# Other places for the split weights of the merge stage, unread products at the start, and some loads issued earlier or by another queue

## The chip, the cores and the metric

The kernel runs on one core of a Trainium2 chip. PE multiplies: a matmul takes a stationary operand of 128 x 128, its weights, which a weight load (PEld in the profile) brings in beforehand, and streams a moving operand of up to 512 columns past it into a PSUM bank. DVE and ACT do elementwise work, POOL and SP mostly issue DMAs here. Each engine works through its own list of instructions in order, and semaphores tie the lists together. The order on each list is not written by hand throughout: a scheduler makes it when the program is built, from the order of the Python calls and from which operands it expects to be ready.

The metric is the device time of one execution in microseconds (us). The kernel before takes 2859.32 us, the median of 3 runs (2859.23 to 2859.35).

## The reference

One encoder block over 512 tokens of 2048 channels, all in float32. Cut to what matters here:

```
hn = rmsnorm(x, norm1_w);  proj = hn @ w_in            # 2048 -> 11280 columns
conv_out = centred_depthwise_conv(proj[:, :5120])
y_a = hyena(conv_out[:, :3072])          # long convolutions with a learned filter
y_b = sigmoid(o) * mlstm_both_directions(q, k, v, gates)
gate_a, gate_b = sigmoid(merge[:, :2048]), sigmoid(merge[:, 2048:])
mixed = gate_a * (y_a @ w_branch_a) + gate_b * (y_b @ w_branch_b)
x = x + mixed @ w_out
gu = rmsnorm(x, norm2_w) @ w_gate_up
x = x + (silu(gu[:, :5632]) * gu[:, 5632:]) @ w_down
return rmsnorm(x, norm_f_w)
```

`merge` is the last 4096 columns of `proj`. It is 16 groups of 256 columns, and these groups are the merge stage.

## The kernel before

**Products in float32 by splitting.** Every operand is split into a high part, rounded to the type that PE takes in one pass (F32R), and a low part, the remainder. A product is three matmuls: high x high, high x low, low x high (`mm3`, L78 to L81, all through `mm`, L75 to L76). A split is an ACT copy (the high part) and a DVE subtraction (the low part): L176 and L177 in `split_w`, L1105 and L1106 in the class `Winograd`, L86 and L87 in `split`.

**Stages, in order.** At the start `x` is loaded, transposed by PE and split into the 16 pairs of `X` (pool `ap`, tiles `a`). Then the main stream works through the columns of `w_in` in groups of 256 (`w_in_cols`), with matmuls of 512 columns. Beside it runs a side stream, of which `drive` takes a few pieces at each tick of the main stream: the Hyena convolutions (`hyena`), the mLSTM heads (`mlstm`) and the filter spectra. The merge stage follows, then `branch_a` and `branch_b`, the output projection, the gate-up stage and the down projection.

**The start** (L304 to L349). `x` comes in five pieces of columns (256, 256, 512, 512, 512), each in four tiles `xt`, all loaded by SP's queue. The first weights (`raws`, tiles `wr` of 512 KB, L169) stand in the same queue behind pieces 0, 2 and 3. `x_block(kb)` transposes one block of 128 columns (L320) into a PSUM tile `sd`, `x_split` scales and splits it (L326, L327), and after every two blocks one unit of the first column group runs, 12 matmuls of 512 columns. The pool of `sd` tiles has four buffers.

**Heads and convolutions.** `stream_a` runs `hyena(0)`, `hyena(1)`, `mlstm(0)`, `hyena(2)`, `hyena(3)` and then heads 1 to 3. A head runs eight units, one for each direction and block of 128 tokens; each makes its weights by ACT, a mask on POOL (`affine_select`, L955), DVE and ACT again. `hyena(q)` takes tiles that were fetched ahead if there are any (`fetched`); otherwise it issues four loads from `d_hy` on POOL's queue (`fetch`, L823) and pauses for two ticks. Its first PE work is the transposes of `by_times` (L759). A head fetches the `q` and `k` of the next head at its sixth unit (`following`); `mlstm(0)` is called without it.

**The merge stage.** `Winograd.cols` makes 256 columns in seven products of 8 x 3 matmuls of 256 columns, 168 in all. It takes a weight block apart into quarters, makes four sums of quarters (`add`, L1122), and splits every quarter and sum that a product needs, in two tiles of 4 x 128 columns each. So a group has 14 pairs of split tiles and 8 sum tiles. The moving operands are the tiles `a` and the combinations `T` (pool `ts`).

**Where the tiles lie.** Pools on the left side are laid one above the other from low addresses, those on the right side are counted down from the top, which stands 32 bytes below a multiple of 64. The left pools of this stage, `wp` (tiles `wr`, `wh`, `wl`), `ap` and `ts`, start at multiples of 64 bytes. All the tiles of the stage are 2048 or 4096 bytes in a partition (`xo`, `bt` and `tt` included), so those on the right lie at 32 modulo 64. In the merge stage before, split tiles are taken in turn: four pairs in `wp` (`wh`, `wl`), then two in right pools of their own (`h`, `l`); the sums are six tiles `s` on the right. The gate-up stage is the same class; there pools named `tpx`, `w2x` and `h2x`, which hold nothing, move the `T` tiles 32 bytes up against the split weights, which are four pairs in `wp` and one more.

The right pools of the merge stage take over the memory of the pool `pr`, whose tiles the column groups and the side stream use (`g`, `st`, `pp`). A new tile waits until the tiles under it have been used for the last time (`reuse_waits="tile"`). The last group ahead of the merge stage, `o_cols`, stores two `st` tiles to `d_o` by POOL's queue (L457).

**`branch_a`** loads, once per group, one tile of `d_yb` and one of `d_o` by SP's queue (`load_tile`, L1255), multiplies them a group later and splits them for `branch_b`.

Of the kernel before, what the change touches and what calls it, by code (L numbers as in the profile page):

```python
# [8 lines left out]
F32 = mybir.dt.float32  # L9
# [25 lines left out]
def hybrid_block_kernel(ctx, tc, x, norm1_w, w_in, conv_w, conv_b, filt_w1, filt_b1, filt_freq1,  # L35
# [268 lines left out]

    pieces = [(0, 256), (256, 256), (512, 512), (1024, 512), (1536, 512)]
    xt = [[new(xp, f"xt{c}_{tb}", (P, n)) for tb in range(4)] for c, (_, n) in enumerate(pieces)]
    raws = []
    for c, (c0, n) in enumerate(pieces):
        for tb in range(4):
            nc.sync.dma_start(xt[c][tb], x2d[tb * P:(tb + 1) * P, c0:c0 + n])  # L310
        if c in (0, 2, 3):
            raws.append(load_a(w_in, len(raws) * L, 0))
    first_group = group_feat(w_in, 0, KB, 0, X, raws)

    def x_block(kb):
        ps = sd_ps()
        c = max(i for i, (c0, _) in enumerate(pieces) if c0 <= kb * P)
        k0 = kb * P - pieces[c][0]
        for tb in range(4):
            nc.tensor.transpose(ps[:, tb * P:(tb + 1) * P], xt[c][tb][:, k0:k0 + P], ident)  # L320
        return ps

    def x_split(kb, ps):
# [3 lines left out]
        nc.vector.scalar_tensor_tensor(l, ps, n1[:, kb:kb + 1], h.bitcast(F32), ALU.mult, ALU.subtract)  # L327
        X[kb] = (h, l)

    for kb in range(0, KB, 2):  # L330
        blocks = [x_block(kb), x_block(kb + 1)]
        if kb == 0:
            small_columns()
        if kb:
            next(first_group)
        for k in range(2):
            x_split(kb + k, blocks[k])
# [550 lines left out]
    def mlstm(h, following=None):  # L888
# [82 lines left out]
        for n, (d, jb) in enumerate(units):  # L971
            if n == 4:
                W = {}
            if n == 5 and ("qk", following) in done:
                fetched_qk[following] = fetch_qk(following)
            W[jb] = nxt
            if n < 7:
                nxt = weights(*units[n + 1], row if n < 3 else row_b)
# [32 lines left out]
    def stream_a():  # L1011
        yield from gate_rows()
        yield from need("filter")
        for kind, n in (("hy", 0), ("hy", 1), ("hd", 0), ("hy", 2), ("hy", 3)):
            yield from hyena(n) if kind == "hy" else mlstm(n)
        ph_cm.__exit__(None, None, None)
        ts_pool.append(ts_cm.__enter__())
        done.add("ts")
        for h in (1, 2, 3):
            yield from mlstm(h, h + 1)  # L1020

    def stream_b():
        yield from filter_net()
# [200 lines left out]
        n_tile[0] += 1  # L1224
        return sx.tile(list(shape), F32, tag="bt", name=f"bt_{n_tile[0]}", bufs=4)

    wm_cm = {t: tc.tile_pool(name="wm" + t, bufs=b, side="right", reuse_waits="tile") for t, b in (("r", 4), ("s", 6), ("h", 2), ("l", 2))}
    wm = {t: cm.__enter__() for t, cm in wm_cm.items()}
    d_g = [[dram(f"d_g{k}_{b}") for b in range(16)] for k in range(2)]

# [4 lines left out]
    def ring(tag, shape, dt, own, pool, extra, more):  # L1235
# [7 lines left out]
            return new(pool, extra, shape, dt)  # L1243
        return take

    merge = Winograd(
        w_in, XT, ring("wr", (P, 4, 256), F32, 3, wm["r"], "r", 4),
        ring("wh", (P, 4, P), F32R, 4, wm["h"], "h", 2), ring("wl", (P, 4, P), F32R, 4, wm["l"], "l", 2),
        lambda: new(wm["s"], "s", (P, 4, P)), xo, lambda: bt((P, 256)))

    ya, yb = [], []

# [16 lines left out]
            nc.scalar.activation(C[j], C[j], AF.Sigmoid)  # L1269
            nc.gpsimd.dma_start(dst[j], C[j])  # L1270

    for t in ("l", "h", "s", "r"):
        wm_cm[t].__exit__(None, None, None)
    ts_cm.__exit__(None, None, None)
    pg_cm = tc.tile_pool(name="pg", bufs=20, reuse_waits="tile")
# [11 lines left out]
    def branch_a():  # L1287

        raw = []

        def put_yb():
            t, o = raw.pop(0)
            nc.vector.tensor_tensor(t, t, o, ALU.mult)
            yb.append(split(py, "y", t))

        for g in range(8):
            gates_g = [gate_tile(0, 2 * g + j) for j in range(2)]
            for r in group_feat(w_branch_a[0], 0, 8, g * 256, ya):
                if r is None:
                    yield  # L1300
            for j in range(2):
                nc.vector.tensor_tensor(gates_g[j], r[j], gates_g[j], ALU.mult)
                acc.append(gates_g[j])
            if raw:
                put_yb()
            raw.append((load_tile(d_yb, g, nc.sync), load_tile(d_o, g, nc.sync)))
        put_yb()

    mixed = []
# [295 lines left out]
```

## Time and profile before

| | |
|---|---|
| median of the timed runs | 2859.32 us |
| the profiled execution | 2869.02 us |
| its span, first to last instruction | 2867.3 us |
| DVE, busy | 2104.9 us |
| ACT, busy | 1273.0 us |
| POOL, busy | 186.2 us |
| mean granted TensorE clock | 0.998 |

The profile comes from one execution of its own, which is some 10 us longer than the timed runs. Times inside it are counted from its first instruction. A row of the timeline gives the start, the time of one stretch of like instructions, engine, line, operation, the tiles (written <- read) and, in brackets, how long the engine idled before and what ended that wait. The starts of two matmul rows tell what the matmuls between them cost; a row's own time holds the length of the pipeline as well and is longer. A name without its number stands for all tiles of that name, so `wh` and `h` tell apart two places in memory.

### The profile page before, as it was taken

The page shows a single profiled execution, that of the slowest core. Times are in us where ns is not written, and L with a number is a line of the kernel's source. Part 1 is how long each engine was busy: PE and PEld are TensorE (multiplying, and loading weights), DVE is VectorE, ACT ScalarE, POOL GpSimd, SP SyncE. Part 2 cuts the span into 40 slices and gives each one's busy share as a digit, 9 for nine tenths or more (in the row PEclk, how much of TensorE's full clock was granted, in tenths as well). Part 3 has the DMA queues.
Part 4 walks back from the last instruction along what each step waited for, and adds up shares of the span by engine and source line. Part 5 has one row for each costly group of instructions (what it writes and reads, how often), then busy time and mean ns, then how long its engine had stood idle before and what let it go on. Part 6 is the DMA issues. An engine that isn't in the chain of part 4 may idle for free.

```text
span 2867.3 us, 47431 instructions
## 1 busy us (share of the span) xinstructions
PE 2840.8 (99%) x18028; PEld 2569.3 (90%) x18028; DVE 2104.9 (73%) x3844; ACT 1273.0 (44%) x2259; POOL 186.2 (6%) x431
## 2 busy tenths in 40 slices
PE   9999999999999999999999999999999999999998
PEld 7888878888899999888899999999999998888886
DVE  6898869888588888554459889888898885233336
ACT  5434453446645545223445444444444445233224
POOL 0101121012100001000010000000000000000000
PEclk9999999999999999999999999999999999999999
DMA  5334443344344445643443343334333336343433
GB/s 180 115 118 129 125 133 122 110 144 147 114 151 129 133 140 164 223 140 109 136 142 118 124 127 122 115 115 128 124 118 118 120 102 217 96 129 115 126 115 126
DMA packets 281490, 376.97 MB, mean 131 GB/s; under 512 B 18620, under 2 KB 214660, under 8 KB 281261
## 3 DMA queue, kind: packets, MB, share of 16 engines
q1 hardware_dynamic: 257243, 298.36, 34.0%
q0 software_dynamic: 22752, 73.44, 7.6%
q8 instruction: 141, 2.31, 0.3%
q10 hardware_dynamic: 1266, 2.13, 0.2%
q14 instruction: 88, 0.72, 0.1%
HBM read 326.67 MB, written 47.20 MB: 130 GB/s over the span
## 4 chain that ended last, share of the span: by engine, by line
PE 71%; DVE 1%; DMA 0%; ACT 0%; issue 0%; ACTq 0%
PE mm L76 50%; PE sd L76 21%; DMA wr<-in_w_down_dram 0%; PE sd L1364 0%; DVE h L87 0%; DVE T L1392 0%; DVE s L1122 0%; ACT h L86 0%; DVE wl L177 0%; DVE wl L1106 0%; PE sd L998 0%; DVE x L1532 0%; ACT sq L1535 0%; ACT x L1544 0%; DVE g L957 0%
## 5 line engine op out<-in xcount | busy, mean ns | idle before, releaser
L177 DVE TENSOR_TENSOR wl<-wr,wh 128x512 fp32r<-128x512 f32 x512 | 350.8, 689 | 452.8 <-ACT wh L176 444.7
L176 ACT CAST wh<-wr 128x512 fp32r<-128x512 f32 x512 | 316.7, 622 | 739.1 <-PE mm L76 674.3
L76 PE MATMUL mm<-a,wh 128*128 128x512 f32 (+1 forms) x2128 | 620.8, 375 | 0.4 <-ACT wh L176 0.4
L76 PEld LDWEIGHTS mm<-a,wh 128*128 128x128 f32 x2128 | 386.1, 189 | 67.5 <-ACT wh L176 0.8
L76 PE MATMUL mm<-T,wh 128*128 128x256 f32 x2232 | 401.2, 282 | 2.8 <-ACT T L1391 2.3
L76 PE MATMUL mm<-a,wl 128*128 128x512 f32 (+1 forms) x1064 | 398.2, 374 | 1.0 <-DVE wl L177 1.0
L76 PE MATMUL sd<-T,wh 128*128 128x256 f32 x2224 | 397.6, 281 | 0.0
L76 PE MATMUL mm<-wh,h 128*128 128x512 f32 x1280 | 394.7, 389 | 1.1 <-ACT h L86 1.1
L76 PEld LDWEIGHTS mm<-T,wh 128*128 128x128 f32 x2232 | 341.7, 189 | 3.4 <-ACT T L1391 2.5
L1105 ACT CAST wh<-s 128x512 fp32r<-128x512 f32 x365 | 226.8, 622 | 253.3 <-PE sd L76 123.5
L76 PEld LDWEIGHTS sd<-T,wh 128*128 128x128 f32 x2224 | 339.1, 188 | 0.0
L76 PE MATMUL mm<-T,wl 128*128 128x256 f32 x1116 | 311.8, 279 | 0.3 <-DVE wl L1106 0.3
L76 PE MATMUL sd<-T,wl 128*128 128x256 f32 x1112 | 310.0, 279 | 0.0
L76 PEld LDWEIGHTS mm<-wh,h 128*128 128x128 f32 x1280 | 240.3, 188 | 51.3 <-ACT h L86 1.3
L1106 DVE TENSOR_TENSOR wl<-s,wh 128x512 fp32r<-128x512 f32 x365 | 249.9, 686 | 11.5 <-ACT wh L1105 8.1
L76 PE MATMUL mm<-wl,h 128*128 128x512 f32 x640 | 249.1, 389 | 0.0
L76 PE MATMUL mm<-wh,a 128*128 128x512 f32 (+1 forms) x896 | 247.2, 360 | 0.0
L76 PEld LDWEIGHTS mm<-a,wl 128*128 128x128 f32 x1064 | 201.0, 189 | 35.8 <-DVE wl L177 1.4
L76 PEld LDWEIGHTS mm<-T,wl 128*128 128x128 f32 x1116 | 211.1, 189 | 0.5 <-DVE wl L1106 0.5
L76 PEld LDWEIGHTS sd<-T,wl 128*128 128x128 f32 x1112 | 209.8, 189 | 0.0
L76 PEld LDWEIGHTS mm<-wh,a 128*128 128x128 f32 x896 | 160.3, 189 | 24.6
L76 PE MATMUL mm<-wl,a 128*128 128x512 f32 (+1 forms) x448 | 161.0, 359 | 0.0
(368 smaller groups left out, 4776.3 us busy)
## 6 DMA issues: line engine op xcount, KB each, us to landing
wr<-in_w_in_dram SPq DMA_DIRECT2D x140, 512.0 KB, 3.6
r<-in_w_gate_up_dram SPq DMA_DIRECT2D x100, 512.0 KB, 4.6
wr<-in_w_down_dram SPq DMA_DIRECT2D x88, 512.0 KB, 3.7
wr<-in_w_gate_up_dram SPq DMA_DIRECT2D x76, 512.0 KB, 4.2
r<-in_w_in_dram SPq DMA_DIRECT2D x36, 512.0 KB, 4.5
wr<-in_w_out_dram SPq DMA_DIRECT2D x32, 512.0 KB, 3.6
d_h<-xo POOLq DMA_DIRECT2D x44, 256.0 KB, 2.6
hl<-d_h SPq DMA_DIRECT2D x44, 256.0 KB, 3.5
```

The costliest lines, as they stand in the source:

```text
L76: nc.tensor.matmul(o, a, b, start=start, stop=stop)
L176: nc.scalar.copy(h, src)
L177: nc.vector.tensor_tensor(l, src, h.bitcast(F32), ALU.subtract)
L1105: nc.scalar.copy(h, a)
L1106: nc.vector.tensor_tensor(l, a, h.bitcast(F32), ALU.subtract)
```

## The change

Four parts, and nothing else is touched.

1. Merge stage: the first two pairs of split tiles come from `wp`, all others from right pools of five high and five low tiles (`split_tile`). The sums take the places `wh` and `wl` of `wp` in turn, eight in all (`sum_tile`); the pool `s` is gone. The four `r` tiles for raw weights remain.
2. Start: the first 512 KB of weights come as two loads of 256 KB, behind pieces 0 and 1 of `x`. PE gets products whose results nobody reads: six plain float32 products of a tile of ones ahead of everything, and two and six further transposes of the `x` tile at hand behind the last two transposes of block 1. They write a PSUM tile `unread` of the pool of `sd`.
3. `mlstm(0)` fetches the four tiles of `hyena(2)` at its sixth unit, if they have been stored by then; heads 1 to 3 do what they did.
4. `branch_a` loads `d_yb` and `d_o` by POOL's queue in place of SP's.

```diff
-    raws = []
+    raws = [wp.tile([P, 4, 256], F32, tag="wr", name="wr_0", bufs=3)]
     for c, (c0, n) in enumerate(pieces):
         for tb in range(4):
             nc.sync.dma_start(xt[c][tb], x2d[tb * P:(tb + 1) * P, c0:c0 + n])
-        if c in (0, 2, 3):
+        if c < 2:
+            nc.sync.dma_start(raws[0][:, 2 * c:2 * c + 2, :],
+                              w_in[2 * c * P:(2 * c + 2) * P, 0:256].rearrange("(k p) c -> p k c", p=P))
+        elif c < 4:
             raws.append(load_a(w_in, len(raws) * L, 0))
...
+    unread = sd_ps()
+    def idle(n, a=None):
+        for _ in range(n):
+            if a is None:
+                mm(unread[:, 0:P], onesf, onesf, True, True)
+            else:
+                nc.tensor.transpose(unread[:, 0:P], a, ident)
...
             nc.tensor.transpose(ps[:, tb * P:(tb + 1) * P], xt[c][tb][:, k0:k0 + P], ident)
+            if kb == 1 and tb > 1:
+                idle((2, 6)[tb - 2], xt[c][tb][:, k0:k0 + P])
...
+    idle(6)
     for kb in range(0, KB, 2):
...
-            if n == 5 and ("qk", following) in done:
-                fetched_qk[following] = fetch_qk(following)
+            if n == 5 and following in done:
+                kind, m = following
+                if kind == "qk":
+                    fetched_qk[m] = fetch_qk(m)
+                else:
+                    fetched[m] = fetch(m, 0), fetch(m, 1)
...
-            yield from hyena(n) if kind == "hy" else mlstm(n)
+            yield from hyena(n) if kind == "hy" else mlstm(n, ("hy", 2))
...
-            yield from mlstm(h, h + 1)
+            yield from mlstm(h, ("qk", h + 1))
...
-for t, b in (("r", 4), ("s", 6), ("h", 2), ("l", 2))}
+for t, b in (("r", 4), ("h", 5), ("l", 5))}
...
+    def sum_tile():
+        n_sum[0] += 1
+        return wtile("wh" if n_sum[0] % 2 else "wl", [P, 4, P], F32, 4)
+    def split_tile(t):
+        n = [0]
+        def take():
+            n[0] += 1
+            if n[0] <= 2:
+                return wtile("w" + t, [P, 4, P], F32R, 4)
+            return new(wm[t], t, (P, 4, P), F32R)
+        return take
     merge = Winograd(
         w_in, XT, ring("wr", (P, 4, 256), F32, 3, wm["r"], "r", 4),
-        ring("wh", (P, 4, P), F32R, 4, wm["h"], "h", 2), ring("wl", (P, 4, P), F32R, 4, wm["l"], "l", 2),
-        lambda: new(wm["s"], "s", (P, 4, P)), xo, lambda: bt((P, 256)))
+        split_tile("h"), split_tile("l"), sum_tile, xo, lambda: bt((P, 256)))
...
-            raw.append((load_tile(d_yb, g, nc.sync), load_tile(d_o, g, nc.sync)))
+            raw.append((load_tile(d_yb, g, nc.gpsimd), load_tile(d_o, g, nc.gpsimd)))
```

More of the change, by code (lines that the diff above doesn't have):

```diff
@@ L1225, in bt @@
         return sx.tile(list(shape), F32, tag="bt", name=f"bt_{n_tile[0]}", bufs=4)
-    wm_cm = {t: tc.tile_pool(name="wm" + t, bufs=b, side="right", reuse_waits="tile") for t, b in (("r", 4), ("s", 6), ("h", 2), ("l", 2))}
+    wm_cm = {t: tc.tile_pool(name="wm" + t, bufs=b, side="right", reuse_waits="tile") for t, b in (("r", 4), ("h", 5), ("l", 5))}
     wm = {t: cm.__enter__() for t, cm in wm_cm.items()}
@@ L1244, in ring @@
         return take
+    n_sum = [0]
+    def sum_tile():
[9 more added lines that the diff above has]
+        return take
     merge = Winograd(
         w_in, XT, ring("wr", (P, 4, 256), F32, 3, wm["r"], "r", 4),
-        ring("wh", (P, 4, P), F32R, 4, wm["h"], "h", 2), ring("wl", (P, 4, P), F32R, 4, wm["l"], "l", 2),
-        lambda: new(wm["s"], "s", (P, 4, P)), xo, lambda: bt((P, 256)))
+        split_tile("h"), split_tile("l"), sum_tile, xo, lambda: bt((P, 256)))
     ya, yb = [], []
@@ L1270, in hybrid_block_kernel @@
             nc.gpsimd.dma_start(dst[j], C[j])
-    for t in ("l", "h", "s", "r"):
+    for t in ("l", "h", "r"):
         wm_cm[t].__exit__(None, None, None)
```

## The prediction

> **What bounds the kernel now.** I read the page's first part, then the chain of waits, then the wait totals of PE, then the timeline where PE waits.
>
> ```profile
> PE 2840.8 (99%) x18028; PEld 2569.3 (90%) x18028; DVE 2104.9 (73%) x3844; ACT 1273.0 (44%) x2259; POOL 186.2 (6%) x431
> ```
> ```profile
> 838.43 20.00 PE sd L76 x168
> 858.42 19.93 PE mm L76 x168
> ...
> 1138.03 217.63 PE mm L76 x960
> ...
> 1525.48 19.79 PE sd L76 x168
> ```
> ```profile
> PE sd L320 <- DMA xt<-in_x_dram: 6.3, 3, 4.1
> ...
> PE sd L759 <- DMA g<-d_hy: 1.2, 1, 1.2
> ...
> PE mm L76 <- DVE wl L1106: 0.3, 1, 0.3
> ```
>
> PE is busy for 2840.8 of 2867.3 us, so the time can fall in two ways only: a wait of PE goes, or a matmul takes less. The second block (start, us, what) shows the merge stage, one group of 168 matmuls per row: 15 groups from 838.43 to 1138.03, 299.60 us, so 19.97 each. A gate-up group of the same 168 matmuls takes 19.79. The third block (us in total, times, longest) holds the PE waits that the change touches.
>
> **Merge stage: split weights.** Within one merge group the weights come from two places. Tiles `wh`, `wl` lie in the left pool `wp`, at a multiple of 64 bytes like the moving operands `a` and `T`. Tiles `h`, `l` lie in right pools, which are counted down from an end 32 bytes short of a multiple of 64, all in pieces of 2048 or 4096 bytes. So they already lie 32 bytes below the moving operands, modulo 64.
>
> ```profile
> 838.26 0.40 PE L76 MATMUL sd<-a,wh 128*128 128x256 f32 x2
> ...
> 841.14 0.40 PE L76 MATMUL sd<-a,h 128*128 128x256 f32 x2
> ...
> 843.95 0.40 PE L76 MATMUL sd<-a,wh 128*128 128x256 f32 x2
> ```
>
> From 838.26 to 841.14 run 24 matmuls on `wh` and `wl`: 2.88 us, 120.0 ns each. From 841.14 to 843.95 run 24 on `h` and `l`: 2.81 us, 117.1 ns each. All else is the same: moving `a`, 256 columns, no wait. That is the effect to be extended, already present in this stage. A group has 14 pairs of split tiles, 16 groups 224; the rotation of 4 + 2 puts a third of them into `h`, `l`. After the change all but the first two are there: 224 x 2/3 - 2 = 147 pairs move, 12 matmuls each, 0.035 us a pair. **147 x 0.035 = 5.1 us less.** Bounds: the two rows are rounded to 0.01 us, so 0.05 to 0.09 per 24, 3.7 to 6.6 us.
>
> The Trainium skill speaks against this term: "TensorE: Matmul & The Clock Gate", "Step-by-step: what each phase is for", says that PE reads weights and the moving operand through two independent SBUF ports, so that loading the next weights takes nothing from the running matmul. By that the place of the weights is worth nothing and the term is 0; the two stretches above differ all the same.
>
> What could take it back: the split pairs in rotation fall from 6 to 5, the sums rise from 6 tiles to 8.
>
> ```profile
> 838.43:1138.03 299.60, 299.60 (x2521) 299.60 (x2521) 263.27 (x468) 154.42 (x263) 20.36 (x39) 1.00 0.44 135
> 1525.48:2356.52 831.04, 831.04 (x7058) 831.04 (x7058) 746.91 (x1306) 401.93 (x675) 22.70 (x42) 1.00 0.39 121
> ```
>
> Columns: window, length, then PE, PEld, DVE, ACT, POOL. Merge has DVE at 263.27/299.60 = 88%; with 5.1 us less it is 89%. Gate-up runs the same class with 4 + 1 = 5 pairs and 6 sums at 90% DVE without a wait of PE. I cost the smaller ring at 0.
>
> **Entry to the merge stage.** The third pair is the first to lie in the new place. The pool of `l` is the lowest of the right pools, and its first tile overlaps by 32 bytes the last `st` tile of `o_cols`, whose store to `d_o` must have ended.
>
> ```profile
> 820.81 0.40 PE L76 MATMUL mm<-a,wh 128*128 128x256 f32 x2
> 821.05 0.28 PE L76 MATMUL mm<-a,wl 128*128 128x256 f32 x1
> ```
> ```profile
> 819.88 0.54 POOL L457 DMA_DIRECT2D d_o<-st  x1 [0.65 <-ACT st L456]
> ```
> ```profile
> L177 DVE TENSOR_TENSOR wl<-wr,wh 128x512 fp32r<-128x512 f32 x512 | 350.8, 689 | 452.8 <-ACT wh L176 444.7
> ```
> ```profile
> DMA to landing us min/median/max: 2.3/2.4/5.7
> ```
>
> PE wants that pair's lower half at 821.05. The store is issued at 819.88 and lands 2.3 later, at 822.2; a split then takes DVE 0.69 (689 ns, L177). So PE may wait from 821.05 to 822.9, 1.9 us, in place of the 0.3 for DVE L1106. Bounds: 0 if a product that is ready runs first, 3 if the sums behind it on DVE come late too. **I take 1.2 us more**, between, since the order already mixes two products at this place.
>
> **Start.** Here PE waits for `x`, and then runs slowly.
>
> ```profile
> 4.06 1.14 PE L320 MATMUL sd<-csm,xt 128*128 128x128 f32 x4 [4.06 <-DMA xt<-in_x_dram]
> ...
> 6.97 0.69 PE L320 MATMUL sd<-csm,xt 128*128 128x128 f32 x2 [1.23 <-DMA xt<-in_x_dram]
> 8.64 0.69 PE L320 MATMUL sd<-csm,xt 128*128 128x128 f32 x2 [0.99 <-DMA xt<-in_x_dram]
> 9.70 0.80 PE L76 MATMUL mm<-a,wh 128*128 128x512 f32 x1 [0.36 <-ACT wh L176]
> ...
> 13.28 0.63 PE L76 MATMUL mm<-a,wl 128*128 128x512 f32 x1
> 13.71 1.00 PE L76 MATMUL mm<-a,wh 128*128 128x512 f32 x2
> 14.54 0.39 PE L76 MATMUL mm<-a,wl 128*128 128x512 f32 x1
> 14.77 0.63 PE L76 MATMUL mm<-a,wh 128*128 128x512 f32 x2
> ...
> 19.12 1.03 PE L320 MATMUL sd<-csm,xt 128*128 128x128 f32 x8
> ...
> 22.74 1.03 PE L320 MATMUL sd<-csm,xt 128*128 128x128 f32 x8
> ```
>
> From 13.28 to 13.71 a matmul of 512 columns takes 0.43, from 14.54 to 14.77 it takes 0.23; in steady state 960 of them take 217.63, so 0.227. PE's clock is at half until about 14.5. A full round (8 transposes, 12 matmuls) takes 22.74 - 19.12 = 3.62 at full clock: 12 x 0.227 + 8 x 0.11. Between 9.70 and 19.12 lie 24 such matmuls and 14 transposes, 7.0 us at full clock, and 9.42 pass: **2.4 us are lost to the half clock**.
>
> The unread products fill the waits ahead of 9.70. Six plain float32 products, two instructions each, cost about 0.24 at full clock, as this row shows (the next PE row starts at 42.92), so about 0.5 cold and 2.9 together, inside the 4.06 of idling. Eight transposes at twice 0.11 (1.7 us) lie in the waits of 1.23 and 0.99.
>
> ```profile
> 42.68 0.49 PE L76 MATMUL sd<-csm,rb 128*128 128x128 f32 x2
> ```
> ```profile
> 3.61 4.99 SPq L310 DMA_DIRECT2D xt<-in_x_dram  x8
> ```
> ```profile
> xt<-in_x_dram SPq DMA_DIRECT2D x12, 256.0 KB, 6.0
> ```
>
> PE is then occupied from about 1 to 9.7 with gaps, so the clock should be up by 11.1. What is late next is `x`: the third piece is issued until 8.6 and lands 6.0 later at the median, so its transposes (now up to 16.4) can't come before about 13.5 to 14.5. **I take 2.2 us less.** Bounds: 0.5 us more (the clock opens no earlier and the extra transposes stand in front of real ones); 4.0 less (the first weights, half as large ahead of the second piece of `x`, also bring the first matmul up to 1.4 us forward). The extra DMA costs SP one issue, 0.6 (4.99 for 8), and no bytes.
>
> The Trainium skill, same page, "What's actually happening", puts the opening of the clock after about 3.4 us of sustained activity; by that it would open near 4.5 to 5 and the term would be the full 2.4. That agrees with the sum but for 0.2.
>
> **Fetch ahead in `mlstm`.**
>
> ```profile
> 397.81 0.54 POOL L415 DMA_DIRECT2D d_hy<-st  x1 [2.19 <-DVE st L405]
> ...
> 413.98 0.57 POOL L823 DMA_DIRECT2D g<-d_hy  x1
> 418.78 1.08 POOL L1001 DMA_DIRECT2D d_yb<-g  x2 [4.23 <-ACT g L1000]
> 419.86 1.63 POOL L823 DMA_DIRECT2D g<-d_hy  x3
> ```
> ```profile
> 424.75 0.87 PE L759 MATMUL sd<-csm,g 128*128 128x128 f32 x6 [1.16 <-DMA g<-d_hy]
> ```
>
> The last store that `hyena(2)` needs is issued at 397.81, 21 us before head 0's own results are stored (418.78), and in the program's order its mark is set one tick ahead of head 0's fifth unit. So the test at the sixth finds it, and the fetch does move forward. Its four issues, 0.54 each, then stand on POOL ahead of two masks of the units that follow; head 1 to 3 have the same four issues there today and no long PE wait. The wait of 1.16 goes; the two pauses go too, which moves side work forward, and that work is not what ends last. **1.2 us less**, bounds 1 more (masks 2.2 us late on POOL) and 2.5 less.
>
> **Loads of `d_yb` and `d_o` by POOL's queue.** PE has no gap from 1138.03 on for 217.63, so SP's queue costs nothing there, and POOL (6%) has room for 16 issues of 0.54. Each tile is used a group, some 27 us, later. 0.
>
> **Sum.** -5.1 + 1.2 - 2.2 - 1.2 = -7.3 us: the span goes from 2867.3 to 2860.0. The profiled execution took 2869.02 in all, the timed runs 2859.32; 9.7 us belong to the profiling or to waits that are shorter without it. I take the difference over unchanged: **2852.0**. From the bounds that pull one way the gain is 1 to 14; independent, about 4 to 11.
>
> **Rivals.**
>
> One, **the clock's dip after the output projection moves.**
>
> ```profile
> 1499.30:1502.72 3.42, 2.79 (x20) 2.11 (x18) 3.42 (x9) 3.33 (x10) 0.00 (x0) 1.00 0.00 0
> 1502.72:1506.13 3.41, 0.89 (x3) 0.48 (x3) 3.41 (x10) 2.27 (x9) 0.00 (x0) 1.00 0.00 0
> 1506.13:1509.54 3.41, 2.45 (x10) 2.23 (x11) 3.41 (x8) 3.09 (x5) 0.00 (x0) 0.50 0.00 0
> 1509.54:1512.96 3.42, 3.42 (x18) 3.42 (x18) 2.81 (x9) 1.90 (x5) 0.00 (x0) 0.50 0.56 158
> ```
>
> The clock is 0.50 for two windows of 3.41 after one with little PE work; PE works 2.45 + 3.42 there, so about 2.9 us are lost. Everything before moves by 7 us, so the idle stretch falls otherwise across such windows: the loss can vanish, or stay. For it: after a window 2.79/3.42 = 82% busy (first row) nothing dropped. Against: the idle stretch is longer than one window. Vanished: 2849.1.
>
> Two, **the start or the entry gives most of it back** (the clock opens late, or DVE's sums pile up behind the third pair): 5.1 + 1.2 - 3 = 3.3 less, 2856.0, within 0.2%.
>
> Three, **the ring of five is too short** (the slower one). DVE is at 89%; if it lags, PE waits for one split, 0.69, at two of the seven products of each group: 16 x 2 x 0.69 = 22 us, less 7.3, is 15 more, 2874. It decides from the point at which a product's two splits and its sum (3 x 0.69) don't fit into its 2.8 us beside DVE's evacuation. Gate-up speaks against it.
>
> Four, **the address is not the cause** (the two ports of the skill's page; something else than the place makes `h`, `l` faster): 1.2 + 2.2 - 1.2 = 2.2 less, 2857.1.
>
> **How the numbers follow.** Forecast (2850 to 2853.5) 0.55, first rival 0.17, second 0.18, third 0.05, fourth 0.05. A measurement can tell some 0.2%, 5.7 us, from no change. Faster by more: 0.55 + 0.17 = 0.72. Within: 0.18 + 0.05 = 0.23. Slower: 0.05. The range for 8 in 10 leaves out the third and fourth rival and the ends of the others: 2847.5 to 2856.0.
>
> **What would show it.** Merge groups at 19.65 to 19.70 each and the names `h`, `l` throughout: the main term. A group at 19.97: the fourth rival. PE waits on L1106 in every group: the third. Two rows 0.227 apart for 512 columns before 12 us: the start. No wait of PE at L759: the fetch. A PE wait of 1 to 2 us some 3 us after the first merge matmul: the entry. The forecast is wrong if the groups stay above 19.85 or if the start shifts by less than 1 us.

## The result, and the profile after

The changed kernel takes 2869.47 us (median of 9 runs, 2867.12 to 2878.74), the kernel before 2859.47 beside it: 1.0035 times as long, with an interval of 1.0024 to 1.0045. It is **slower by 0.35%**, about 10 us, where 7.3 less were forecast.

The profiled execution took 2878.74 us, 9.7 more than that of before, and its span is 2877.0. Line numbers behind the start are shifted: L1126 and L1127 are the old L1105 and L1106, L1143 is the sum (old L1122), L334 the transposes of `x` (old L320), L1332 the product of `d_yb` and `d_o`. First part of the page, then the chain of waits (start, us, what):

```profile
PE 2844.6 (99%) x18048; PEld 2569.0 (89%) x18048; DVE 2111.4 (73%) x3844; ACT 1267.8 (44%) x2255; POOL 194.7 (7%) x447
```
```profile
816.90 2.27 DMA d_o<-st
819.26 4.47 DMA r<-in_w_in_dram
824.43 18.32 PE mm L76 x132
842.74 19.60 PE sd L76 x168
862.34 19.60 PE mm L76 x168
...
1135.16 6.25 DMA bt<-d_o
...
1142.50 5.89 DMA bt<-d_o
...
1157.11 8.90 DMA bt<-d_o
...
1175.85 187.52 PE mm L76 x826
...
1532.73 19.79 PE sd L76 x168
```

The merge groups are at 19.60, better than forecast, so the main term of the change arrived. But the chain, which ran over PE here but for two short pieces of DVE at 822, now goes through a raw load at 819.26 and through loads of `d_o` from 1135 on. PE's waits (us in total, times, longest) name the same two places; the 3.4 for the split weights of `branch_a` (L176) and the 3.7 for `h` (L1126) are new, the wait at the transposes of `hyena(2)` is gone:

```profile
PE mm L76 <- ACT h L1126: 4.5, 2, 3.7
PE mm L76 <- ACT wh L176: 3.4, 2, 3.2
...
PE mm L76 <- DVE x L1542: 1.8, 1, 1.8
PE sd L334 <- DMA xt<-in_x_dram: 1.4, 3, 0.7
```

The waits are shorter than the loss. Windows of the clock (columns as before) show the rest:

```profile
819.94:823.35 3.41, 0.74 (x7) 0.54 (x5) 0.00 (x0) 0.00 (x0) 0.00 (x0) 1.00 1.02 328
823.35:826.76 3.41, 2.33 (x10) 2.32 (x11) 3.00 (x5) 1.14 (x2) 0.00 (x0) 0.50 1.08 356
826.76:830.17 3.41, 3.41 (x18) 3.41 (x17) 3.24 (x6) 2.47 (x5) 0.00 (x0) 0.50 0.68 191
1161.27:1164.68 3.41, 0.78 (x3) 0.35 (x3) 1.99 (x3) 1.14 (x2) 0.95 (x2) 1.00 1.05 393
1164.68:1168.09 3.41, 3.41 (x8) 2.76 (x9) 1.30 (x3) 1.14 (x2) 0.66 (x2) 0.50 1.06 413
```

In each place a window in which PE worked 0.74 or 0.78 of 3.41 us is followed by one or two at half the clock. A wait of 3 to 4 us thus costs 1.7 us (one window with PE busy) to 2.9 us (2.33 + 3.41, halved) more behind it. In `branch_a` the waits (3.4 for L176, 1.1 for L177) and the clock make 6.2 of the loss of 9.0 in the table below; the rest are delays of 0.1 to 0.3 us between single matmuls from 1150 to 1176.

Where the time went, stage by stage. Each length is the distance of the starts of the same two matmuls in both timelines, so the rows add up to the difference of the profiled executions, but for 0.1 behind the last matmul:

| stretch | before | after | difference |
|---|---|---|---|
| first instruction to one matmul early in the side stream | 47.10 | 43.84 | -3.3 |
| from there to the merge stage | 770.84 | 771.11 | +0.3 |
| merge group 1 | 20.32 | 27.63 | **+7.3** |
| merge groups 2 to 16 | 299.60 | 294.00 | -5.6 |
| `branch_a` | 87.07 | 96.07 | **+9.0** |
| `branch_b`, output projection, first gate-up group | 300.39 | 299.91 | -0.5 |
| gate-up | 852.10 | 852.10 | 0.0 |
| down projection but for its last 160 matmuls | 443.59 | 446.20 | +2.6 |
| those | 36.27 | 36.26 | 0.0 |

### The profile page after: what moved, and what is told of

Read it like the earlier page. It is cut to its first block, busy times and chain, and to the rows that moved or that the text cites. A ratio compares the mean times of both kernels' runs of the same rounds, so it can differ in the third digit from the quotient of the medians.

```text
span 2877.0 us, 47482 instructions
## 1 busy us (share of the span) xinstructions
PE 2844.6 (99%) x18048; PEld 2569.0 (89%) x18048; DVE 2111.4 (73%) x3844; ACT 1267.8 (44%) x2255; POOL 194.7 (7%) x447
## 4 chain that ended last, share of the span: by engine, by line
PE 68%; issue 2%; DMA 2%; DVE 1%; ACT 0%; POOL 0%; POOLq 0%; DVEq 0%; SPq 0%; ACTq 0%
PE mm L76 47%; PE sd L76 20%; DMA bt<-d_o 1%; DMA wr<-in_w_down_dram 0%; PE sd L1403 0%; DVE h L87 0%; DVE T L1431 0%; DMA r<-in_w_in_dram 0%; DMA bt<-d_ya 0%; DVE bt L1332 0%; DVE s L1143 0%; ACT h L1126 0%; POOL d_o L474 0%; ACT y L86 0%; ACT h L86 0%
## 5 line engine op out<-in xcount | busy, mean ns | idle before, releaser
L177 DVE TENSOR_TENSOR wl<-wr,wh 128x512 fp32r<-128x512 f32 x512 | 350.5, 688 | 455.8 <-ACT wh L176 446.7
L176 ACT CAST wh<-wr 128x512 fp32r<-128x512 f32 x512 | 317.1, 622 | 736.3 <-PE mm L76 672.9
L76 PE MATMUL mm<-a,wh 128*128 128x512 f32 (+1 forms) x1808 | 563.0, 391 | 3.4 <-ACT wh L176 3.4
L76 PEld LDWEIGHTS mm<-a,wh 128*128 128x128 f32 x1808 | 335.8, 188 | 71.5 <-ACT wh L176 5.0
L76 PE MATMUL mm<-T,wh 128*128 128x256 f32 x1976 | 354.4, 281 | 2.8 <-ACT T L1430 2.3
L76 PE MATMUL mm<-a,wl 128*128 128x512 f32 x904 | 353.5, 391 | 1.3 <-DVE wl L177 1.1
L76 PE MATMUL sd<-T,wh 128*128 128x256 f32 x1968 | 351.1, 280 | 0.0
L76 PEld LDWEIGHTS mm<-T,wh 128*128 128x128 f32 x1976 | 301.3, 188 | 3.4 <-ACT T L1430 2.5
L76 PEld LDWEIGHTS sd<-T,wh 128*128 128x128 f32 x1968 | 299.0, 188 | 0.0
L76 PE MATMUL mm<-T,wl 128*128 128x256 f32 x988 | 275.3, 279 | 0.3 <-DVE wl L1127 0.3
L1126 ACT CAST wh<-s 128x512 fp32r<-128x512 f32 x281 | 174.7, 623 | 198.3 <-PE sd L76 96.9
L1127 DVE TENSOR_TENSOR wl<-s,wh 128x512 fp32r<-128x512 f32 x281 | 192.6, 686 | 8.2 <-ACT wh L1126 4.4
```

Of the source, the lines that this page charges most:

```text
L76: nc.tensor.matmul(o, a, b, start=start, stop=stop)
L176: nc.scalar.copy(h, src)
L177: nc.vector.tensor_tensor(l, src, h.bitcast(F32), ALU.subtract)
L1126: nc.scalar.copy(h, a)
L1127: nc.vector.tensor_tensor(l, a, h.bitcast(F32), ALU.subtract)
```

## The two theories

**Group 1.** SP's timeline (start, us, queue, line, load, count), before and after:

```profile
799.00 10.17 SPq L1114 DMA_DIRECT2D wr<-in_w_in_dram  x3
809.40 2.16 SPq L1114 DMA_DIRECT2D r<-in_w_in_dram  x4
827.42 3.34 SPq L1114 DMA_DIRECT2D wr<-in_w_in_dram  x3
```
```profile
794.71 24.32 SPq L1135 DMA_DIRECT2D wr<-in_w_in_dram  x4
819.26 2.41 SPq L1135 DMA_DIRECT2D r<-in_w_in_dram  x4
```

A group has four raw loads. Before, group 1 takes three `wr` and one `r`, and the next three `r` belong to group 2; only then comes group 2's `wr`. After, a fourth `wr` stands ahead of the first `r`. It is group 2's, takes over the memory of group 1's first raw tile, and so waits for the last sums that read that tile, as the waits of SP's queue in this stretch say:

```profile
SPq L1135 <- DVE wh L1143: 12.4, 1, 12.4
```

Group 1's own fourth load stands behind it in order and goes out at 819.26, not at 809.40; its landing is the 4.47 of the chain, and ACT, idle for it since 817, makes `h` from it at 823.75. The order is the scheduler's: with eight places for sums, so I read it, it has no reason to expect the last sums of group 1 late. **Theory: that order costs the 7.3. Rival: the store to `d_o`**, which the prediction expected under the third split tile and which the chain puts just ahead of the `r` load.

**`branch_a`.** ACT's list of the program, from the first high part of `y` (`*`) to the last, with the weight splits `wh` and others between:

```
before  * xo wh wh * wh wh * wh wh * wh wh * wh * wh wh * wh *
after   * xo wh * wh * wh * wh * wh * wh * wh *
```

A `y` waits for two loads, a product and the `bt` tiles of the one before. A `wh` feeds 12 matmuls of 512 columns, 2.7 us of PE. ACT's timeline after has it so:

```profile
1155.47 0.62 ACT L86 CAST y<-bt 128x512 fp32r<-128x512 f32 x1 [2.17 <-DVE bt L1332]
1155.99 0.62 ACT L176 CAST wh<-wr 128x512 fp32r<-128x512 f32 x1
1162.63 0.62 ACT L86 CAST y<-bt 128x512 fp32r<-128x512 f32 x1 [6.02 <-DVE bt L1332]
1163.16 0.61 ACT L176 CAST wh<-wr 128x512 fp32r<-128x512 f32 x1
```

Between the weight splits at 1155.99 and 1163.16 lie 7.2 us, since a `y` waits for 6.02 of them in front of the second, which itself has nothing to wait for. From 1143.83 to 1170.99 ACT makes 7 weight splits, 19 us of work for PE in 27. **Theory: the order on ACT's and DVE's lists. Rivals: POOL's queue lands the loads late; or the merge stage's new end.**

## The experiments

Each was measured beside the kernel before, which had medians of 2859.5 to 2860.5 in these comparisons. Lengths are taken from the traces as above.

| kernel | early matmul | to merge | group 1 | 2 to 16 | `branch_a` | gate-up | down | median | ratio, interval |
|---|---|---|---|---|---|---|---|---|---|
| before | 47.10 | 770.84 | 20.32 | 299.60 | 87.07 | 852.10 | 443.59 | | |
| after | 43.84 | 771.11 | 27.63 | 294.00 | 96.07 | 852.10 | 446.20 | 2869.47 | 1.0035, 1.0024 to 1.0045 |
| e1 merge alone | 45.94 | 770.49 | 27.82 | 294.00 | 87.44 | 852.09 | 443.68 | 2862.89 | 1.0010, 1.0001 to 1.0019 |
| e2 start alone | 43.52 | 770.39 | 20.32 | 299.60 | 87.07 | 844.07 | 444.78 | 2859.45 | 1.0003, 0.9992 to 1.0014 |
| e3 queue alone | 46.27 | 770.69 | 20.32 | 299.60 | 98.31 | 844.07 | 443.60 | 2870.65 | 1.0041, 1.0028 to 1.0055 |
| e4 late sums, SP's loads | 44.34 | 771.45 | 19.96 | 294.00 | 87.10 | 852.10 | 446.87 | 2854.94 | 0.9984, 0.9974 to 0.9995 |
| e5 unread products only | 44.05 | 770.85 | 20.32 | 299.60 | 87.07 | 844.08 | 444.93 | 2860.24 | 1.0001, 0.9992 to 1.0010 |
| e6 e4, SP's count kept | 43.69 | 771.28 | 20.09 | 296.80 | 87.31 | 844.07 | 445.19 | 2856.40 | 0.9987, 0.9978 to 0.9996 |
| e7 fetch alone | 45.73 | 770.41 | 20.32 | 299.60 | 87.84 | 844.07 | 443.74 | 2859.96 | 0.9999, 0.9990 to 1.0008 |
| e8 `d_yb` by SP | 46.02 | 770.64 | 20.32 | 299.60 | 96.85 | 844.08 | 443.29 | 2868.73 | 1.0032, 1.0020 to 1.0044 |
| e9 merge, late sums | 46.01 | 771.41 | 22.04 | 294.00 | 88.58 | 844.07 | 443.53 | 2858.04 | 0.9996, 0.9988 to 1.0005 |
| e10 e9 and start | 43.75 | 771.17 | 22.03 | 294.00 | 87.06 | 852.09 | 444.52 | 2856.76 | 0.9996, 0.9986 to 1.0005 |
| e11 e10, filler of 32 | 43.44 | 772.40 | 20.02 | 296.79 | 87.09 | 844.07 | 444.71 | 2856.07 | 0.9994, 0.9984 to 1.0004 |
| e12 paced loads | 46.34 | 770.51 | 20.33 | 299.60 | 87.25 | 844.07 | 443.95 | 2860.65 | 1.0003, 0.9995 to 1.0012 |
| e13 e10, filler of 224 | 43.83 | 771.63 | 20.24 | 302.40 | 87.06 | 844.07 | 444.49 | 2861.47 | 1.0012, 1.0003 to 1.0021 |
| e14 e10, filler of 96 | 43.81 | 771.00 | 20.11 | 299.05 | 87.05 | 844.07 | 444.65 | 2857.90 | 0.9995, 0.9983 to 1.0006 |

Gate-up takes 852.1 in some executions and 844.1 in others, in kernels that do not differ there. A time of one execution says little unless this is known; the profiles of before and after both have 852.1. The lengths of a kernel come from one execution each.

### One part at a time

**e1**, the merge stage's part on the kernel before:

```diff
-(("r", 4), ("s", 6), ("h", 2), ("l", 2))
+(("r", 4), ("h", 5), ("l", 5))
...
+        split_tile("h"), split_tile("l"), sum_tile, xo, lambda: bt((P, 256)))
```

> Only the merge stage's part of the change (split tiles and sums in other places) on the kernel before. Theory, the order of SP's queue: with eight places for the sums the last two sums of group 1 no longer wait for a place, so the scheduler puts group 2's first raw load, which waits for one of these sums, ahead of group 1's fourth raw load, and this one comes late. Then group 1 takes 25 to 28 us (20.32 in the kernel before, 27.63 in the changed one), with PE waiting some 3 to 4 us for a split of the fourth load and a half clock behind it; groups 2 to 16 take 19.60 each (19.97 before), 5.5 us less in all; branch_a keeps its 87.1 us; the time is 1 to 2 us above the kernel before. Rival, the store under the third split tile: the fourth raw load is issued at about 809 as before, only the third pair waits, 1 to 2 us, and group 1 takes 21 to 22: the time is 3 to 4 us below the kernel before.

Group 1 takes 27.82, groups 2 to 16 take 294.00: the part gives 5.6 and takes 7.5 by itself. SP's timeline has the order of the changed kernel, and PE waits for both, the fourth load (`h`) and the third pair (`l`):

```profile
797.49 23.02 SPq L1114 DMA_DIRECT2D wr<-in_w_in_dram  x4
820.74 2.09 SPq L1114 DMA_DIRECT2D r<-in_w_in_dram  x4
```
```profile
PE mm L76 <- ACT h L1105: 3.3, 1, 3.3
PE mm L76 <- DVE l L1106: 1.8, 1, 1.8
```

The load goes out at 820.74, so the rival in its pure form (issued at 809) falls.

**e2**, the start's part (halves and unread products) on the kernel before:

```diff
+            nc.sync.dma_start(raws[0][:, 2 * c:2 * c + 2, :],
...
+    idle(6)
```

> Only the start's part (weights in halves, unread products) on the kernel before. Theory: the clock is granted in full from about 4 us on, the matmul that started at 49.48 starts at 46.2 to 47, and what is won is kept: the merge stage's first matmul comes at 814.8 to 816 (817.94 before), the time falls by 2 to 3.3 us. Rival, given back: the side stream ends no earlier or the clock dips elsewhere, so that the merge stage begins at 817 to 818 and the time is that of the kernel before within 1 us.

The early matmul comes at 43.52 and the merge stage's first at 813.91, 2.5 to 3 us earlier than in e1 and e3. But the ratio of 1.0003 has 1 within its interval, so the fall of 2 to 3.3 us that was expected is not shown; the down projection has 1.2 more than before. More on it at e6.

**e3**, the loads by POOL's queue on the kernel before:

```diff
-            raw.append((load_tile(d_yb, g, nc.sync), load_tile(d_o, g, nc.sync)))
+            raw.append((load_tile(d_yb, g, nc.gpsimd), load_tile(d_o, g, nc.gpsimd)))
```

> Only the loads of d_yb and d_o by POOL's queue, on the kernel before. Theory: the loads are placed otherwise, so that the products and splits that wait for them stand on DVE and ACT in front of splits of branch_a's weights; PE then waits three times or so, 2 to 4 us each, for a split in wh, with a half clock behind. From branch_a's first matmul to branch_b's first pass 93 to 97 us (87.07 before, 96.07 in the changed kernel), and the time rises by 6 to 9.5 us. Rival, the earlier and other end of the merge stage costs it: 87 us for branch_a, the time of the kernel before.

`branch_a` takes 98.31, somewhat over what was expected, and the kernel is 0.41% slower. The merge stage of before ends where it did, so that rival falls. **This one line, costed at 0, costs by itself as much as the whole change loses** (the two intervals overlap).

**e7**, the early fetch alone:

```diff
+            if n == 5 and following in done:
...
-            yield from hyena(n) if kind == "hy" else mlstm(n)
+            yield from hyena(n) if kind == "hy" else mlstm(n, ("hy", 2))
```

> Only the early fetch in mlstm(0), on the kernel before. From the matmul that starts at 47.1 to the merge stage's first the kernels without it took 770.4 to 770.8 us, the two with it 771.1 and 771.4. Theory: the wait for d_hy at the transposes of hyena(2) is gone and the side stream runs into other waits, so that this stretch is 771.0 to 771.6 and the time 0 to 1 us longer. Rival, the prediction's: the stretch falls to 769.3 to 770, the time by 0.5 to 1.5 us.

770.41 us to the merge stage, where the six other kernels without the merge stage's part show 770.39 to 770.85. Neither the small loss nor the gain of 1.2 is there. PE's wait at L759 is no longer for the load:

```profile
PE sd L759 <- DVE g L872: 0.5, 1, 0.5
```

### Group 1: the order and the overlap

**e4**, the changed kernel with SP's loads in `branch_a` and the last two sums of group 1 elsewhere:

```diff
         n_sum[0] += 1
+        if n_sum[0] in (7, 8):
+            t = "h" if n_sum[0] == 7 else "l"
+            return new(wm[t], t, (P, 4, P), F32)
...
-            raw.append((load_tile(d_yb, g, nc.gpsimd), load_tile(d_o, g, nc.gpsimd)))
+            raw.append((load_tile(d_yb, g, nc.sync), load_tile(d_o, g, nc.sync)))
```

> The changed kernel with two edits: d_yb and d_o are loaded by SP again, and the last two sums of merge group 1 take an h and an l tile of the right pools, so that they wait for their place as they did before. The third split pair stays where the changed kernel has it, over the st tile whose store must end. Theory, the order of SP's queue: the fourth raw load of group 1 goes out by about 810 or earlier, ahead of group 2's first, nothing waits for its split, and group 1 takes 20 to 21.5 us, the rest of it a wait of up to 1 us for the third pair; branch_a takes 87; with 3 us from the start and 5.5 from groups 2 to 16 the time is 7 to 9 us below the kernel before, 2850.5 to 2852.5. Rival, the store under the third pair: group 1 keeps 23 to 27 us, and the time is 1 to 5 us below the kernel before.

```profile
795.54 11.47 SPq L1135 DMA_DIRECT2D wr<-in_w_in_dram  x3
807.24 2.22 SPq L1135 DMA_DIRECT2D r<-in_w_in_dram  x4
```

Three `wr`, then the `r` at 807.24; group 1 takes 19.96 and PE waits for nothing in the merge stage. Where two sums lie decides over 7.7 us. The last store to `d_o` is issued at 817.73 here, 10 us behind the `r` load, so the load does not wait for it, although the chain of the changed kernel has the store ahead of it. The time, 0.9984 of before with its interval below 1, is the lowest of the study, not told apart from e6's 0.9987: **a version that beats both kernels.** Of the 7 to 9 us expected 3.3 are missing in the down projection.

**e9** and **e10** take the same late sums without the fetch, and without or with the start:

```diff
-            yield from hyena(n) if kind == "hy" else mlstm(n, ("hy", 2))
+            yield from hyena(n) if kind == "hy" else mlstm(n)
```

> Of the change only the merge stage's part, with the last two sums of group 1 in an h and an l tile. Theory: SP's order is that of the kernel before, group 1 takes 19.9 to 20.4 us (27.82 with the part as it stands), groups 2 to 16 take 294.0 or, in an execution of the other kind that one run has shown, 296.8 (299.6 before), nothing else moves: the time is 2.8 to 6 us below the kernel before. Rival, the sums in right pools stall later groups: over 297.

> The merge stage's part with the two late sums and the start's part; no early fetch, and d_yb and d_o by SP. Theory: start some 2.4 us earlier (first column at 43.5 to 44.3), merge groups 2 to 16 at 294.0 or 296.8, branch_a 87, and the stall at the end of the down projection at 1.9 to 2.5 us again as in all five kernels with unread products (0.5 to 1.0 in the five without): in sum 4 to 7.5 us below the kernel before. Rival, the parts take away from each other elsewhere: within 2 us of the kernel with the merge stage's part alone or above it.

Both have SP's order right and still take 22.0 for group 1, a miss, and neither time is told apart from that of before. The chain of e9:

```profile
818.17 0.54 POOL d_o L457
...
819.36 2.39 DMA d_o<-st
...
821.85 0.70 DVE l L1106
...
822.60 17.03 PE mm L76 x142
```

This is the prediction's overlap step by step: the store to `d_o`, its landing, the low part that waits for it, PE idle for 1.9 us. Why not in e4? In e9 and e10 the last `st` tile starts at byte 171968, and the first `l` tile covers 169952 to 172000: 32 bytes in common. In the kernels with the early fetch the same pool hands out its places in another turn and the last `st` starts at 174016. The tile under `l` there is that of an earlier store, issued at 795.88 in e4.

**e11** moves the right pools down by 32 bytes, which also takes that overlap away:

```diff
+    wmx_cm = shifted("wmx", 8, side="right")
```

> The kernel with merge stage and start, and under the right pools of the merge stage a filler of 32 bytes, so that all its split tiles there lie at a multiple of 64 bytes like the moving operands; pools, rotation and order stay. Theory, the address: all 14 pairs of a group run at 120.0 ns a matmul, 168 of them 20.16 us, groups 2 to 16 take 301 to 302.4 us, 5 to 8.4 more than with the 32 bytes, and the time rises by as much. Rival, the pools of their own and not the address: 294 to 297 and no change.

Group 1 takes 20.02: the 2 us of e10 are the overlap. What the run was made for came out the other way, see below.

### `branch_a`: the lists

**e8**, one of the two loads by POOL:

```diff
-            raw.append((load_tile(d_yb, g, nc.sync), load_tile(d_o, g, nc.sync)))
+            raw.append((load_tile(d_yb, g, nc.sync), load_tile(d_o, g, nc.gpsimd)))
```

> On the kernel before, d_o by POOL's queue and d_yb by SP's. In ACT's list the eight high parts of y then have two, two, one, one, one, one weight splits between them from the third on, where the kernel before has two in all but two of these places and the kernel with both loads on POOL one in all. Theory, the lists: a y needs a round trip of some 8 us and PE uses a weight split in 2.7, so the stall of branch_a lies between the two, 90 to 96 us for the stretch that took 87.07 and 98.31; the time rises by 3 to 8 us. Rival, the landing by POOL's queue is what is slow: the d_o loads take longer to land than SP's, and the stretch is 96 to 99 as with both. Second rival, two queues at once overlap the two loads: 87 to 88.

96.85, above what was expected and at the edge of the rival: this run doesn't decide. One `y` waits 10.85 us in it, longer than in the other kernels of this section; why stays open. Late landings do occur: the `d_o` loads of the stage, with POOL's queue in the changed kernel, and with SP's in e1 (of eight loads two have a known landing there):

```profile
DMA to landing us min/median/max: 3.8/5.6/8.9
```
```profile
DMA to landing us min/median/max: 5.7/7.7/9.8
```

In the changed kernel a load that landed 8.0 us after its issue stands behind the wait of 6.02 above. But in e1 `branch_a` takes 87.44, so a landing of 9.8 us by itself costs almost nothing, and late landings are no mark of POOL's queue.

**e12**, both by POOL, but each load behind a result of the stage:

```diff
+    def load_paced(src, g):
+        t = bt()
+        nc.vector.tensor_copy(t[:, 0:1], acc[2 * (g // 2)][:, 0:1])
+        nc.gpsimd.dma_start(t, src[g])
+        return t
...
-            raw.append((load_tile(d_yb, g, nc.sync), load_tile(d_o, g, nc.sync)))
+            raw.append((load_paced(d_yb, g), load_paced(d_o, g)))
```

> On the kernel before, d_yb and d_o both by POOL's queue as in the change, but each load waits for the result of a group of branch_a (a copy of one column into the tile ahead of the load), groups 0 and 1 for that of group 0, 2 and 3 for group 2 and so on, so that in ACT's list 16 weight splits stand between the first and the last y, as against 7 in the kernel with both loads on POOL and 11 in the kernel before. Theory, the lists: branch_a takes 87 to 89 us and the time is that of the kernel before to 1 us above. Rival, POOL's queue or its landing: 93 to 99, 6 to 11 us above.

87.25, no wait of PE in the stage, with all 16 loads on POOL's queue. (The kernel before has 12 weight splits there, as its list above shows, not 11, and e12 has 13, not 16.) Nor do the waits of `y` on ACT tell the kernels apart: the longest is 6.28 us in the kernel before and 7.41 in e12, where PE loses nothing, and 6.02 in the changed kernel. **The queue by itself is not the cause; what fits all these runs is what the lists hold between two `y`.** That the scheduler set them close because on POOL they no longer stand behind SP's weight loads is argued, not shown.

### The address

e11 was to give 120.0 ns a matmul if a multiple of 64 bytes were the rule. It gave 296.79, so the rule that the prediction read is wrong or too narrow: with 32 bytes of filler the tiles still lie 64 bytes from the moving operands modulo 256. **e13** and **e14** take fillers of 224 and 96 bytes:

```diff
-    wmx_cm = shifted("wmx", 8, side="right")
+    wmx_cm = shifted("wmx", 56, side="right")
```

> As the kernel with 32 bytes of filler, but with 224: all split tiles in the merge stage's right pools then start at a multiple of 256 bytes, as the moving operands and the tiles of wp do, one under the other modulo 256. Theory, the address modulo 256 (the filler of 32 bytes left the tiles 64 bytes below the moving operands): 120.0 ns a matmul, groups 2 to 16 take 301 to 302.4 us, 5 to 8 more than with the other fillers. Rival, pools of their own in high memory, whatever the address: 294 to 297.

> The same with 96 bytes of filler: the split tiles lie 128 bytes from the moving operands modulo 256. If equality modulo 256 makes the slow pitch: groups 2 to 16 at 294.0 or 296.8 as with 32 and 64 bytes. If equality modulo 128 does: 301 to 302.4. Pools alone: 294 to 297, and the kernel with 224 bytes the same.

One group of e13, of e14, of e11 and of e10, which has no filler, in the chain of waits:

```profile
835.86 20.16 PE sd L76 x168
```
```profile
835.09 19.94 PE sd L76 x168
```
```profile
836.02 19.79 PE sd L76 x168
```
```profile
837.12 19.60 PE sd L76 x168
```

Pools, rotation and order are the same in the four but for the filler. Equal to the moving operands modulo 256 a matmul of 256 columns takes 20.16 / 168 = 120.0 ns, 128 bytes off 118.7, 64 off 117.8, 32 off 116.7. So it is the address: pools of their own give nothing where the addresses are equal modulo 256, and the time of e13 says the same (1.0012, its interval above 1). Three things stay open. e14 lies between its two expected values, so the distance matters by steps and not as a plain yes or no; tiles equal modulo 256 are equal modulo 512 too in these programs, so these two aren't told apart; nor are 64 and 32 bytes, since e6 has 117.8 at 32 as well. The Trainium skill ("TensorE: Matmul & The Clock Gate", "Step-by-step: what each phase is for") gives weights and moving operand a port each, independent of each other; by that the four rows would be alike. They are not, and the measurement decides.

### The end of the down projection

**e5**, the unread products without the halves:

```diff
+    idle(6)
     for kb in range(0, KB, 2):
```

> Of the start's part only the unread products, with the first weights in one load as before. Theory: the open clock is what wins, so the matmul that started at 43.5 to 44.3 in the three kernels with the whole part (45.9 to 47.1 in those without) starts at 44 to 45; SP's queue issues as many loads as the kernel before (688), and the stall at the end of the down projection, 1.9 to 2.5 us in the three kernels with one load more and 0.8 in the three without, is 0.8. From the first row of the last stage's 192 matmuls back to the first of the 44 gate-up groups that follow it, the tail takes 443.6. Rival, the unread products themselves shift the tail: 1.9 us or more; second rival, the halves bring the start forward: then the start here is at 45.5 or later.

The early matmul comes at 44.05, against a mean of 43.8 in the eight kernels that have the halves too and 46.2 in the seven that have neither: of 2.4 us the halves give some 0.3, within the scatter of the eight (43.44 to 44.34). The down projection takes 444.93, so the count of SP's loads, which is that of before here, is not what lengthens it.

**e6**, e4 with one more load taken off SP:

```diff
-        nc.sync.dma_start(rows_a, conv_w[0].rearrange("k (b p) -> (k b) p", p=P))
+        nc.gpsimd.dma_start(rows_a, conv_w[0].rearrange("k (b p) -> (k b) p", p=P))
```

> The kernel with the late sums (d_yb and d_o by SP, two sums of group 1 in right pools) and one load of the start, rows_a, moved from SP's queue to POOL's, so that SP issues 688 loads as the kernel before does, in place of 689. Theory, the count: with the queue's turn of eight as before, the stall at the end of the down projection goes from 2.5 back to 0.8 us and the half clock behind it goes; all other stages stay as they were in the kernel with the late sums: the time falls by some 3 us against it, to 7 to 9.5 below the kernel before. Rival, the earlier start or the fetch moves the tail: the stall stays at 1.9 to 2.6, the time at 5 to 6.5 below.

445.19 and a stall of 2.5: my theory of the count fell twice. The 1.7 between e4 (446.87) and e6, with the same stall, are one window of 3.41 us at half the clock, which follows the stall in e4 and in the changed kernel alone. What stays is a regularity: the nine kernels with unread products take 444.5 to 446.9 here (mean 445.1), the seven without 443.3 to 444.0 (mean 443.6), though the lists of ACT, DVE, SP and POOL are the same in e5 and before from end to end. The chains name a load of `wr`, in the kernel before and in e5:

```profile
2806.09 5.08 DMA wr<-in_w_down_dram
```
```profile
2794.05 6.33 DMA wr<-in_w_down_dram
```

It takes 4.9 to 5.2 us in the seven kernels without unread products and 5.9 to 6.3 in the nine with them; DVE stands behind it with splits ahead of the evacuation that PE waits for. **Why it lands later is open.** The start keeps some 0.9 of its 2.4 us.

## Why the prediction was wrong

- **Merge stage, 5.1 less (3.7 to 6.6): right**, 5.6 in the profile. The ring of five costs nothing, as stated: no PE wait in groups 2 to 16. The reason was nearly right: not 32 bytes modulo 64 but a distance modulo 256 (or 512), of which 32 bytes is the best tried. And e6 shows 296.8 for the same layout, so there the term is 2.8: that the size came out rests in part on luck.
- **Entry, 1.2 more: the step failed.** The prediction asked which memory the third pair takes over, but not what the eight places for sums do to SP's order; of a load that may go out earlier it did not ask what it passes and what it waits for. The loss is 7.3, of which more than 2 lie in the half clock behind the wait. The overlap itself is real (1.9 us in e9, as worked out), but only without the early fetch: one part of the change turned another's tiles, and the parts had been costed one by one. The 0.3 for L1106 that the prediction sets against it is a wait at the start of gate-up; at the entry to the merge stage PE waits for nothing in the kernel before.
- **Start, 2.2 less: right**, 2.4 between the means and 3.3 in the two profiles (the kernel before started latest of all in its own). The clock opened far ahead of the 11.1 of the prediction, as these rows of PE's timeline show:

```profile
1.12 2.93 PE L76 MATMUL sd<-onesf 128*128 128x128 f32 x12 [1.12 <-DVE gb L497]
3.96 0.84 PE L334 MATMUL sd<-csm,xt 128*128 128x128 f32 x4
4.64 0.23 PE L111 MATMUL sd<-csm,rows_b 72*128 72x72 f32 x1
4.87 0.44 PE L334 MATMUL sd<-csm,xt 128*128 128x128 f32 x2
5.14 0.38 PE L327 MATMUL sd<-csm,xt 128*128 128x128 f32 x2
...
9.66 0.39 PE L76 MATMUL mm<-a,wl 128*128 128x512 f32 x1
9.89 0.39 PE L76 MATMUL mm<-a,wh 128*128 128x512 f32 x1
```

Four transposes from 3.96 on take 0.17 each, two from 4.87 on 0.135, and the first two of these wide matmuls with nothing between them stand 0.23 apart, as at full clock.

The end of the down projection, which no step costed, takes 1.5 of it back on the average, 2.6 in this profile.

- **Fetch, 1.2 less: size wrong.** The wait is gone, the stretch is 0.2 shorter, within its scatter. A wait of PE in a side stream that does not end last is not a term of the sum; the prediction said this of the two pauses, not of the wait.
- **`d_yb` and `d_o` by POOL, 0: the step that failed most**, 9.0. It weighed the queues ("SP's queue costs nothing there, and POOL (6%) has room for 16 issues of 0.54") and the time at which each tile is used. It never asked at which place of ACT's and DVE's lists the products and splits stand that wait for these loads, and what is queued behind them. The 27 us were wrong as well: a group of `branch_a` takes 87.07 / 8 = 10.9, and the products come long before a group is over. In the kernel before DVE already stands waiting for such a load, issued 5.6 us earlier at 1150.79:

```profile
1156.39 0.69 DVE L1293 TENSOR_TENSOR bt<-bt,bt 128x512 f32<-128x512 f32 x1 [3.47 <-DMA bt<-d_o]
```

PE having no gap meant that the weight splits came in time, not that they had room.
- **The 9.7 us between profile and median** were put down to the profiling. 8.0 of them are the difference between the two lengths of gate-up, if most timed runs have the shorter one. They seem to: of the nine beside the changed kernel six lie at 2858.2 to 2860.7 and three at 2867.0 to 2868.0.
- **Range and rivals.** The bounds that pull one way add up to 0.8 us of loss and 13.1 of gain, not to gains of 1 and 14. The dip after the output projection stayed, 6.8 us long in both. The second, that start or entry give most back, is the nearest: the entry does give most back, but 7.3 and not 3. The third (ring of five) and the fourth (not the address) fell. The slower outcome came by a way that none of them named.

Without the two failed steps the sum is -5.6 - 2.4 + 1.5 = -6.5, against some -4.6 measured for e4 (0.16% of 2860); the interval, 1.4 to 7.4, holds it. Of the rest, 0.7 may lie in the stretch ahead of the merge stage, which takes 771.3 in the mean of the nine kernels with the merge stage's part (770.5 in e1) and 770.6 in that of the seven without; what costs it wasn't tried.

## What to carry to other kernels

When a load moves to another queue or gets a free buffer earlier, read the in-order lists of every engine that consumes it, and of the queue that it leaves or enters: the cost is what now stands behind a wait there, not the transfer. Cost the parts of a change together where they allocate from the same pools. And add to a wait of PE of 3 us the half clock that followed each of them here.

## What the hardware showed

- Matmuls of 256 columns take 116.7 to 120.0 ns by the distance of weights and moving operand modulo 256 bytes: 3% of a stage for a filler.
- The same instructions take one of two lengths where that distance is 32 bytes: gate-up groups of 19.79 (before, after) or 19.60 (e9, one row below), 8.0 us over the stage, and the merge stage's of 19.79 (e6) or 19.60. The two stages don't change together: e9 has 19.60 in both, e6 19.79 in one. The timed runs of the kernel before lie in two bands some 8 us apart, which fits a change from one execution to the next. What chooses is open.

```profile
1678.32 19.60 PE sd L76 x168
```
- The clock opens earlier when PE gets work earlier, even products of a tile of ones that nobody reads. In the changed kernel they begin at 1.12, the granted clock is full from 4.15 on, and transposes go from 0.17 to 0.135 us (rows of the start above). In the nine kernels with them it is full from between 4.13 and 7.21 on, 3.0 to 6.1 us after they begin, in the seven without from between 12.4 and 14.51. The Trainium skill ("TensorE: Matmul & The Clock Gate", "What's actually happening") puts it after about 3.4 us of sustained activity; the changed kernel agrees with its 3.0, and e4 took 6.1.
